# Where eight row blocks of weight sums are made, and where two squares are taken, in a fused attention and gating layer

## The chip, the cores and the metric

The kernel runs on one core of one Trainium2 chip. The metric is the device time of one launch in microseconds (us), lower is better, and the median of three runs is given. A time taken with the hardware profiler comes from one further execution of its own.

## The reference, cut to what matters

One layer of a trunk with 512 tokens of width 2048, all in float32:

```
hn = rmsnorm(x, norm_g)
q, k, v, gate = split(hn @ w_in)
out = sliding-window attention(q, k, v, with a bias by distance and a sink per head)
x = x + (out * silu(gate)) @ w_out
emb = p @ ple_proj
g = sigmoid(rmsnorm(x, ple_norm) @ ple_gate)
x = x + emb * g
return rmsnorm(x, final_g)
```

`w_out` and `ple_gate` are 2048 x 2048. The change is about the product with `ple_gate`: how some of its weights come about, and when the sums of squares for the norm ahead of it are taken.

## The kernel before, in words

**Products in three passes.** Every float32 operand is split in two: a high part (a cast on ScalarE, ACT) and a low part (a subtraction on VectorE, DVE). A product is then three matmuls: high by high, high by low, low by high (`mm3`, L126 to L128). The weights of `w_out` and `ple_gate` come as blocks of 128 x 1024 numbers, 512 KB each. A block is loaded by SyncE (SP, L757), cast by ACT into `bhi` (L765) and subtracted by DVE into `blo` (L766); then TensorE (PE) uses it in twelve matmuls, or six for the small products. A load of `w_out` goes to one of three buffers (`braw`, tag `wraw`), so it can only be issued when the block three places earlier has been split.

**Six products instead of eight.** The products with `w_out` and with `ple_gate` each multiply 2 x 2 quarters by a scheme that needs seven products of sums of quarters, of which six, numbered 1, 7, 6, 5, 3, 4 in the order of `ORDER_OUT` and `ORDER_PLE`, are done at full size and the seventh by the same scheme again at half size (`Small`). Each product runs over two column halves `jj` and, for each, over four blocks `m`. So a place in the work is written (p, jj, m): (1, 1, 2) is product 1, right columns, third block.

**Sums of weights.** Some products need sums of two or three weight quarters. These are made by DMA, not by an engine: a plain copy from DRAM to DRAM on SP's queue, then a transfer that adds another block to it, on GpSimd's queue (POOL). This goes on all through attention (`sums_in`, `sum_weights`, L723 and L725), up to two copies and two additions in each of 64 iterations `i`. For `ple_gate` there is a second way: the sums of product 7 are loaded from DRAM into eight buffers in SBUF (`seed`, tag `grown`); when product 7 has used such a block, POOL issues a transfer that adds a quarter to the same buffer in place (`grow`, L742), which gives the block of product 6, and later in the same way that of product 4. For the four blocks of product 6's right columns (jj = 1) the kernel before makes the sums in DRAM as well, by copies and additions spread over products 6 and 5 of the `w_out` stage (L1411 and L1414); they are then only loaded over the old block (`again`, L744).

**Stages.** The input projections run interleaved with attention, one iteration of the loop at about 5.6 us, up to about 450 us of the span. Then follows the `w_out` stage up to about 621, and the `ple_gate` stage up to the end. In attention all engines run in the order of the code. In the `w_out` stage PE and SP do, and ACT, DVE and POOL are ordered by the framework's scheduler; from product 4 of `w_out` on ACT is in the code's order too, and from product 7 of `ple_gate` on all are.

**Attention's end.** An iteration `i` has on POOL a small copy (L504), the selection of part of the weights of an earlier iteration (`own`, L575), then the additions of `sum_weights`. The last addition is in iteration 63, the loop runs to iteration 66, and after it POOL issues the first load of `x` (L1027).

**Squares of x.** Once a tile of 128 x 512 of the new `x` is complete, its squares are summed on ACT (L1040). Twelve of the sixteen are put off and taken one at a time at fixed places: four in product 4 of `w_out`, two in (1, 1, 2) and (1, 1, 3) of `ple_gate`, four in (7, 1, 0) to (7, 1, 3), two in (6, 0, 0) and (6, 0, 1). In each place of the stage the order on ACT is: the splits of blocks up to two ahead; then `todo`, with turned tiles scaled into `hT` (L1092), forms of the left operand (`fhg`, L881), a square if one is due; then the forms and blocks of a small product.

Of the kernel before, what the change touches and what calls it, by code (L numbers as in the profile page):

```python
# [11 lines left out]
F32 = mybir.dt.float32  # L12
F32R = mybir.dt.float32r
AF = mybir.ActivationFunctionType
ALU = mybir.AluOpType
# [5 lines left out]
P = 128  # L21
# [34 lines left out]
def trunk_kernel(ctx: ExitStack, tc: tile.TileContext, a: dict):  # L56
    nc = tc.nc
# [28 lines left out]
    WE = 1024  # L86
# [71 lines left out]
    def run(gen):  # L158
        for _ in gen:
            pass  # L160
# [38 lines left out]
    for k in range(KC):  # L199
# [54 lines left out]
        else:  # L254
            high()
            if k == 1:
                src = xw[:, w_at[512] : w_at[512] + 256]
# [9 lines left out]
        f, e = k == 0, k == KC - 1  # L267
# [416 lines left out]
    summed, copies, adds = {}, [], []  # L684

    def block(nm, r, c, jj, m):

        r = r if nm == "w_out" else 3 - r
        return a[nm][2 * (c - 1) + jj, 4 * (r - 1) + m]
# [3 lines left out]
    MORE = {7: (2, 2), 5: (1, 2), 6: (1, 1), 4: (2, 1)}  # L693
# [18 lines left out]
                copies.append((t, block(nm, *BASE[p], jj, m) if p in (7, 5) else summed[nm, BASE[p], jj, m]))  # L712
                adds.append((t, block(nm, *MORE[p], jj, m)))
    sum_small("ple_gate", 4)
    for m in range(4):
        summed["ple_gate", 6, 1, m] = tc.dram_tile([P, WE], F32, name=f"ple_gate_6_1_{m}")
    SUM_STEPS = 2 * len(copies) + 6
    SUMS_EARLY = 16

    def sum_weights(i):  # L720

        if i % 2 == 0 and i // 2 < len(copies):
            nc.sync.dma_start(*copies[i // 2])  # L723
        elif i % 2 == 1 and 0 <= i // 2 - 3 < len(adds):
            nc.gpsimd.dma_start(*adds[i // 2 - 3], accum_op=ALU.add, max_dma_last_dim=8192)  # L725
# [191 lines left out]
    blocks = TWOS * UNITS  # L917

    def sums_in(i):
# [6 lines left out]
        n, of = SUM_STEPS - SUMS_EARLY, blocks - 4  # L926
        return range(SUMS_EARLY + (i - 4) * n // of, SUMS_EARLY + (i - 3) * n // of)

    left = KC * (len(kinds) - 1)

    def some(of, n=1):
# [4 lines left out]
    for i in range(blocks + 3):  # L936

        before, softmax = softmax, scores(i) if i < blocks else iter(())
        turned = turn(i - 2) if 2 <= i < blocks + 2 else iter(())
        value = weigh(i - 3) if 3 <= i else iter(())  # L940
        next(turned, None)
        next(value, None)
        next(softmax, None)
        next(turned, None)
        next(before, None)
        next(softmax, None)
        first_chores(i, 0)
        if i in (6, 20, 36):
            idle.extend(make_key(1 + i // 16))
        todo = left // (blocks + 2 - i) if i < blocks + 2 else 0  # L950
        left -= todo
        for n in range(max(todo, 6)):
            if n < todo:
                next(proj)
            if n == 0:
                first_chores(i, 1)
                some(W.todo)
                some(chores or idle)
            elif n == 2:
                next(turned, None)  # L960
                next(value, None)
                if len(chores) > 1:
                    some(chores)
            elif n == 3:
                next(softmax, None)
            elif n == 4:
                first_chores(i, 2)
                some(chores or idle)
            elif n == 5:
                next(softmax, None)  # L970
        if i < blocks:
            for n in sums_in(i):
                sum_weights(n)
    for _ in proj:
        pass
    while chores or idle:
# [57 lines left out]
    squares_due = []  # L1034
# [338 lines left out]
    sum_copies = [(6, 0, 1), (6, 1, 0), (6, 1, 3), (5, 0, 2)]  # L1373
    sum_adds = [(6, 0, 3), (6, 1, 2), (5, 0, 1), (5, 1, 0)]
# [8 lines left out]
    for n, p in enumerate(ORDER_OUT):  # L1383
        if p == 4:
            last_out.enter_context(
                tc.manual_schedule(
                    engines={getattr(mybir.EngineType, v) for v in ("PE", "SP", "Activation")}
                )
            )
        nxt = out_forms.steps(ORDER_OUT[n + 1]) if n < 5 else iter(())  # L1390
        for jj in range(2):
            later.extend(held.pop(waiting.get((p, jj)), ()))
            calls = iter(range(4))

            def between(m, ps):
                if (p, jj, m) in EMBED_AT:
                    embedding.slot()
                q = small_steps.get((p, jj, m))
                if q is not None:
                    small_out.prepare(q)  # L1400
                for q in SMALL["w_out"].get((p, jj), {}).get(m, ()):
                    small_out.product(q)

            def todo():
                step = next(calls)
                part = x_at.get((p, jj, step))
                if part is not None:
                    load_x(part, nc.sync)
                if (p, jj, step) in sum_copies:
                    m = sum_copies.index((p, jj, step))  # L1410
                    nc.sync.dma_start(summed["ple_gate", 6, 1, m], summed["ple_gate", 7, 1, m])  # L1411
                if (p, jj, step) in sum_adds:
                    m = sum_adds.index((p, jj, step))
                    nc.gpsimd.dma_start(  # L1414
                        summed["ple_gate", 6, 1, m], block("ple_gate", *MORE[6], 1, m), accum_op=ALU.add, max_dma_last_dim=8192
                    )
                part = embed_steps.get((p, jj, step))
                if part is not None:
                    embedding.prepare(part)
                next(nxt, None)  # L1420
                if p == 4:
                    turns_due((p, jj, step))
                    if (jj, step) in ((0, 1), (0, 2), (0, 3), (1, 0)) and squares_due:
                        squares_due.pop(0)()
                if (p, jj) == (4, 1):
                    for _ in range(2 if step >= 2 else 0):
                        turn(*turns.pop(0), "o")
                        next(ple_first, None)

            ps = unit(p, jj, at_out, out_forms, todo, between)  # L1430
            posts = [partial_of(add_y, p, jj, tb, ps[tb]) for tb in range(2)]
            if p == 1:
                held[p, jj] = posts
            elif (p, jj) == (3, 1):
                later.insert(0, lambda both=posts: [post() for post in both])
            else:
                later.extend(posts)
        run(nxt)
        if p == 3:
            turns = [(kp, 0) for kp in range(4)]  # L1440
# [143 lines left out]
    for n, p in enumerate(ORDER_PLE[:-1]):  # L1584
# [9 lines left out]
        for jj in range(2):  # L1594
            calls = iter(range(4))

            def todo():
                nonlocal root_due, fg
                step = next(calls)
                k = early.get((p, jj, step))  # L1600
                if (p, jj, step) in embed_loads:
                    load_embeds(*embed_loads[p, jj, step])
                while small_due:
                    small_due.pop(0)()
                if (p, jj, step) == (5, 0, 2):
                    assert len(moves) == 4
                    while moves:
                        moves.pop(0)()
                if (p, jj, step) == (5, 0, 3):
                    for square in moved.pop(0):  # L1610
                        square()
                if (p, jj, step) == (3, 1, 0):
                    fg = late.tile([P, D], F32, tag="fg", name="fg")
                    nc.sync.dma_start(fg, a["final_g"].partition_broadcast(P))
                if p in (1, 7):
                    turns_due((p, jj, step))
                if (p, jj) == (1, 0):
                    return
                if (p, jj, step) != (7, 0, 0):
                    next(nxt, None)  # L1620
                if p == 1:
                    next(nxt, None)
                if (p, jj, step) == ROOT_AT[0]:
                    assert not squares_due
                    nc.vector.tensor_reduce(ss2, ssq2, axis=AX.X, op=ALU.add)
                    root_due = power_of_mean(rstd2, ss2, "r2")
                    next(root_due)
                if (p, jj, step) == ROOT_AT[1]:
                    run(root_due)
                if (p, jj, step) == (1, 1, 3):  # L1630
                    soon[6] = ple_forms.steps(6)
                    next(soon[6])
                if squares_due and (p == 1 and step > 1 or (p, jj) in ((7, 1), (6, 0))):
                    squares_due.pop(0)()
                if (p, jj, step) == (7, 1, 1):
                    nc.scalar.activation(ss2[:, :1], power[:, :1], AF.Sigmoid)
                if k is not None:
                    split_last(k)
                if (p, jj, step) in opens:
                    open_bank(*opens[p, jj, step])  # L1640
# [30 lines left out]
    f = ple_forms.made[4]  # L1671
# [166 lines left out]
```

## Time and profile before

| | us |
|---|---|
| median of three runs | 781.54 |
| the three runs | 781.34, 781.54, 782.19 |
| the profiled execution, its own time | 781.97 |
| span in that profile, first to last instruction | 780.3 |
| ACT busy, DVE busy, POOL busy | 531.0, 618.9, 169.9 |

The span is what the trace shows, and 781.97 - 780.3 = 1.67 us lie around it. The granted clock of TensorE has a mean of 0.997. Places in the trace are given in us from the span's start. The page of the profile has a line of busy time per engine, tenths of busy time in 40 slices, the DMA queues (q1 carries what SP issues, q0 what POOL issues), the chain of work that ended last, and groups of instructions; further views list who waited for whom, the instructions of an engine in order of time, and busy times and DMA share of chosen stretches. A number in square brackets behind an instruction is the idle time of its engine before it, with what ended it.

### The profile page before, as it was taken

The page shows a single profiled execution, that of the slowest core. Times are in us where ns is not written, and L with a number is a line of the kernel's source. Part 1 is how long each engine was busy: PE and PEld are TensorE (multiplying, and loading weights), DVE is VectorE, ACT ScalarE, POOL GpSimd, SP SyncE. Part 2 cuts the span into 40 slices and gives each one's busy share as a digit, 9 for nine tenths or more (in the row PEclk, how much of TensorE's full clock was granted, in tenths as well). Part 3 has the DMA queues.
Part 4 walks back from the last instruction along what each step waited for, and adds up shares of the span by engine and source line. Part 5 has one row for each costly group of instructions (what it writes and reads, how often), then busy time and mean ns, then how long its engine had stood idle before and what let it go on. Part 6 is the DMA issues. An engine that isn't in the chain of part 4 may idle for free.

```text
span 780.3 us, 11154 instructions
## 1 busy us (share of the span) xinstructions
PE 770.5 (99%) x3652; PEld 644.2 (83%) x3652; DVE 618.9 (79%) x1069; ACT 531.0 (68%) x1121; POOL 169.9 (22%) x307
## 2 busy tenths in 40 slices
PE   9999999999999999999999999999999999999995
PEld 8888888888888888888888888888888888888884
DVE  4556697876978688777877799968799889998995
ACT  6753586766777676766766664577766888866974
POOL 0200523132232313132332200112111122221111
PEclk9999999999999999999999999999999999999998
DMA  8988899999999989999998588999899999999956
GB/s 346 298 216 295 181 275 308 267 307 258 287 250 284 273 238 281 273 279 272 256 285 216 137 304 314 343 300 302 307 388 336 311 292 282 332 258 304 331 135 216
DMA packets 52858, 217.22 MB, mean 278 GB/s; under 512 B 8112, under 2 KB 9136, under 8 KB 46720
## 3 DMA queue, kind: packets, MB, share of 16 engines
q1 hardware_dynamic: 39280, 156.67, 56.5%
q0 software_dynamic: 13520, 59.83, 36.6%
q8 instruction: 29, 0.48, 0.2%
q14 instruction: 29, 0.24, 0.1%
HBM read 199.65 MB, written 82.89 MB: 362 GB/s over the span
## 4 chain that ended last, share of the span: by engine, by line
PE 96%; issue 1%; DMA 1%; ACT 1%; DVE 0%; POOL 0%; POOLq 0%; DVEq 0%; ACTq 0%
PE gps L126 7%; PE gps L127 7%; PE gps L128 7%; PE qps L126 7%; PE qps L128 7%; PE qps L127 7%; PE o L127 6%; PE o L126 6%; PE o L128 6%; PE g L127 4%; PE g L128 4%; PE g L126 4%; PE s L485 2%; PE vps L290 2%; PE o L603 2%; PE pt L551 2%
## 5 line engine op out<-in xcount | busy, mean ns | idle before, releaser
L766 DVE TENSOR_TENSOR blo<-braw,bhi 128x1024 fp32r<-128x1024 f32 x100 | 121.6, 1220 | 21.1 <-ACT bhi L765 20.2
L765 ACT CAST bhi<-braw 128x1024 fp32r<-128x1024 f32 x100 | 105.3, 1054 | 45.1 <-PE o L128 15.0
L126 PE MATMUL gps<-xh,whi 128*128 128x512 f32 x256 | 100.0, 390 | 0.0
L127 PE MATMUL gps<-xl,whi 128*128 128x512 f32 x256 | 99.9, 390 | 0.0
L128 PE MATMUL gps<-xh,wlo 128*128 128x512 f32 x256 | 99.8, 390 | 0.0
L126 PE MATMUL qps<-xh,whi 128*128 128x512 f32 x224 | 87.8, 392 | 0.0
L128 PE MATMUL qps<-xh,wlo 128*128 128x512 f32 x224 | 87.5, 390 | 0.0
L127 PE MATMUL qps<-xl,whi 128*128 128x512 f32 x224 | 87.4, 390 | 0.0
L575 POOL TENSOR_SCALAR_AFFINE_SELECT own<-r 64x512 fp32r<-64x512 f32 (+1 forms) x48 | 32.5, 676 | 238.3 <-DVE r L565 236.1
L110 DVE TENSOR_TENSOR wlo<-wraw,whi 128x1024 fp32r<-128x1024 f32 x60 | 73.5, 1227 | 2.9 <-ACT whi L109 2.7
L126 PE MATMUL o<-bhi,fho 128*128 128x512 f32 x192 | 74.8, 390 | 0.0
L127 PE MATMUL o<-blo,fho 128*128 128x512 f32 x192 | 74.7, 389 | 0.0
L128 PE MATMUL o<-bhi,flo 128*128 128x512 f32 x192 | 74.7, 389 | 0.0
L109 ACT CAST whi<-wraw 128x1024 fp32r<-128x1024 f32 x60 | 62.4, 1042 | 4.6 <-issue 4.1
L127 PE MATMUL g<-blo,fhg 128*128 128x512 f32 x160 | 62.4, 390 | 0.2 <-DVE blo L766 0.2
L126 PE MATMUL g<-bhi,fhg 128*128 128x512 f32 x160 | 62.3, 390 | 0.0
L128 PE MATMUL g<-bhi,flg 128*128 128x512 f32 x160 | 62.3, 389 | 0.0
L128 PEld LDWEIGHTS gps<-xh,wlo 128*128 128x128 f32 x256 | 48.1, 188 | 10.2
L529 ACT ACTIVATE t<-t,sm 128x129 f32<-128x129 f32 (+1 forms) x128 | 50.0, 392 | 8.6 <-DVE sm L525 7.3
L126 PEld LDWEIGHTS gps<-xh,whi 128*128 128x128 f32 x256 | 48.1, 188 | 9.1
L127 PEld LDWEIGHTS gps<-xl,whi 128*128 128x128 f32 x256 | 48.1, 188 | 8.9
L565 DVE TENSOR_TENSOR r<-pt,r 128x256 fp32r<-128x256 f32 x56 | 23.7, 424 | 38.7 <-ACT r L564 37.9
(299 smaller groups left out, 1829.3 us busy)
## 6 DMA issues: line engine op xcount, KB each, us to landing
wraw<-in_w_gate_in SPq DMA_DIRECT2D x32, 512.0 KB, 8.1
w_out<-in_w_out POOLq DMA_DIRECT2D x32, 512.0 KB, 9.1
braw<-w_out SPq DMA_DIRECT2D x32, 512.0 KB, 7.2
wraw<-in_w_q SPq DMA_DIRECT2D x28, 512.0 KB, 6.6
braw<-in_w_out SPq DMA_DIRECT2D x22, 512.0 KB, 5.7
braw<-in_ple_gate SPq DMA_DIRECT2D x22, 512.0 KB, 7.1
ple_gate<-in_ple_gate POOLq DMA_DIRECT2D x20, 512.0 KB, 8.8
xw<-in_first SPq DMA_DIRECT2D x14, 640.5 KB, 6.6
```

The source lines that it names most:

```text
L109: nc.scalar.copy(hi, raw)
L110: nc.vector.tensor_sub(lo, raw, hi.bitcast(F32))
L126: nc.tensor.matmul(ps, sh, mh, start=first, stop=False, skip_group_check=more)
L127: nc.tensor.matmul(ps, sh, ml, start=False, stop=False, skip_group_check=more)
L128: nc.tensor.matmul(ps, sl, mh, start=False, stop=last, skip_group_check=more)
L290: nc.tensor.matmul(v_ps[t], h[:, c], part_of(high_at, 256, 512), start=f, stop=e, skip_group_check=True)
L485: nc.tensor.matmul(s_ps[:, u, : 2 * n], st, of_keys[:, first * 2 * QB : (first * QB + n) * 2], start=True, stop=True)
L529: nc.scalar.activation(su, su, AF.Exp, bias=sm[:, u : u + 1], accum_out=sm[:, 2 + u : 3 + u])
L565: nc.vector.tensor_sub(rl, src, rh.bitcast(F32))
L575: nc.gpsimd.affine_select(out=flat(own), in_=flat(r).bitcast(F32), pattern=[[0, 8], [sign, HB]], compare_op=ALU.is_ge, fill=0.0, base=-HB ...
L765: nc.scalar.copy(hi[:, :n], raw)
L766: nc.vector.tensor_sub(lo[:, :n], raw, hi[:, :n].bitcast(F32))
```

## The change

The four blocks of product 6's left columns (jj = 0) are now made in DRAM too. Their copies are issued by SP at the end of iterations 61 and 62, two in each, and the additions by POOL at the end of iterations 63 to 66, one in each. Since these blocks are then in `summed`, `add_stage` gives them the kind `again`: the four transfers that added to a buffer in place become four plain loads on the same queue. The right columns' copies and additions stay where they were, by way of two new functions. And the two squares of the first product go from steps 2 and 3 of (1, 1) to steps 0 and 3: the first moves two blocks earlier, the second stays. (For (1, 0) `todo` returns before that line.)

```
-    for m in range(4):
-        summed["ple_gate", 6, 1, m] = tc.dram_tile([P, WE], F32, name=f"ple_gate_6_1_{m}")
+    for jj in range(2):
+        for m in range(4):
+            summed["ple_gate", 6, jj, m] = tc.dram_tile([P, WE], F32, name=f"ple_gate_6_{jj}_{m}")
+
+    def copy_six(jj, m):
+        nc.sync.dma_start(summed["ple_gate", 6, jj, m], summed["ple_gate", 7, jj, m])
+
+    def add_six(jj, m):
+        src = block("ple_gate", *MORE[6], jj, m)
+        nc.gpsimd.dma_start(summed["ple_gate", 6, jj, m], src, accum_op=ALU.add, max_dma_last_dim=8192)
+
...
+    six_copied = {blocks - 3: (0, 1), blocks - 2: (2, 3)}
+    six_added = {blocks - 1: (0,), blocks: (1,), blocks + 1: (2,), blocks + 2: (3,)}
...
         if i < blocks:
             for n in sums_in(i):
                 sum_weights(n)
+        for m in six_copied.get(i, ()):
+            copy_six(0, m)
+        for m in six_added.get(i, ()):
+            add_six(0, m)
...
-                if squares_due and (p == 1 and step > 1 or (p, jj) in ((7, 1), (6, 0))):
+                if squares_due and (p == 1 and step in (0, 3) or (p, jj) in ((7, 1), (6, 0))):
                     squares_due.pop(0)()
```

More of the change, by code (lines that the diff above doesn't have):

```diff
@@ L1409, in todo @@
                 if (p, jj, step) in sum_copies:
-                    m = sum_copies.index((p, jj, step))
-                    nc.sync.dma_start(summed["ple_gate", 6, 1, m], summed["ple_gate", 7, 1, m])
+                    copy_six(1, sum_copies.index((p, jj, step)))
                 if (p, jj, step) in sum_adds:
[L1413 to L1416, printed above, removed]
+                    add_six(1, sum_adds.index((p, jj, step)))
                 part = embed_steps.get((p, jj, step))
```

## The prediction

> **What bounds the kernel now.** I read the page first, then the list of who waited for whom, cut to PE, then the chain that ended last.
>
> ```profile
> PE 770.5 (99%) x3652; PEld 644.2 (83%) x3652; DVE 618.9 (79%) x1069; ACT 531.0 (68%) x1121; POOL 169.9 (22%) x307
> ```
>
> ```profile
> PE g L127 <- DVE blo L766: 0.2, 1, 0.2
> ```
>
> ```profile
> 765.00:780.30 15.30, 6.49 (x51) 6.19 (x50) 7.50 (x18) 5.28 (x11) 1.24 (x3) 0.86 0.52 188
> ```
>
> PE is busy for 770.5 of the 780.3 us. Of the 9.8 us that are left, 15.30 - 6.49 = 8.8 lie in the last stretch, after the last matmuls, and most of the rest ahead of the first one. Between them the list names one single wait of PE, 0.2 us, for a low part of weights (`blo`). So an edit that takes no matmul out can win that one wait and little else, while anything that comes too late for PE is paid in full. The rows around it are these, from PE, ACT and DVE in order of time:
>
> ```profile
> 641.29 0.39 PE L126 MATMUL g<-bhi,fhg 128*128 128x512 f32 x1
> 644.01 0.39 PE L126 MATMUL smallg<-bhi,small_ahg 128*128 128x512 f32 x1
> 645.37 0.39 PE L126 MATMUL g<-bhi,fhg 128*128 128x512 f32 x1
> 645.92 0.50 PE L127 MATMUL g<-blo,fhg 128*128 128x512 f32 x1 [0.16 <-DVE blo L766]
> ```
>
> ```profile
> 634.40 0.64 ACT L1163 ACTIVATE small_ahg<-hT 128x512 fp32r<-128x512 f32 x1
> 634.94 1.05 ACT L765 CAST bhi<-braw 128x1024 fp32r<-128x1024 f32 x1
> 638.07 1.05 ACT L765 CAST bhi<-braw 128x1024 fp32r<-128x1024 f32 x1 [1.56 <-DMA braw<-in_ple_gate]
> 642.93 0.63 ACT L1040 ACTIVATE s<-x1s 128x512 f32<-128x512 f32 x1
> 643.56 1.04 ACT L765 CAST bhi<-grown 128x1024 fp32r<-128x1024 f32 x1
> ```
>
> ```profile
> 636.02 1.23 DVE L766 TENSOR_TENSOR blo<-braw,bhi 128x1024 fp32r<-128x1024 f32 x1 [0.18 <-ACT bhi L765]
> 643.17 1.29 DVE L882 TENSOR_TENSOR flg<-hT,fhg 128x512 fp32r<-128x512 f32 x2
> 644.64 1.23 DVE L766 TENSOR_TENSOR blo<-grown,bhi 128x1024 fp32r<-128x1024 f32 x1 [0.18 <-ACT bhi L765]
> ```
>
> Twelve matmuls, one block, take 644.01 - 641.29 = 2.72 us, so one every 0.227. The wait stands where product 7 begins: its first matmul is at 645.37, its second, which needs the low part, at 645.92, 0.55 later and so 0.32 late. The low part came from DVE at 644.64, DVE had waited for the cast at 643.56, and ahead of that cast ACT had taken a square, at 642.93. That square is the one that the change moves.
>
> **The squares.** The first one goes from (1, 1, 2) to (1, 1, 0), where ACT's order puts it straight ahead of the small product's form at 634.40. It takes 643.56 - 642.93 = 0.63 us of ACT. The casts behind it shift by that much, and at 638.07 ACT waits 1.56 us for a load, which swallows it. Who waits for them: the low part at 636.02 would come at about 636.65 and be done at 637.9, for a matmul in the block that starts at 641.29 - 2.72 = 638.57 and needs it 0.23 later: 0.9 us to spare. If that cover were gone it would cost at most 0.63. The squared tile has long been complete: the last addition to `x` is an earlier instruction of DVE, at 614.82, by the same view.
>
> ```profile
> 614.82 0.68 DVE L1120 TENSOR_TENSOR x1s<-smallo,x1s 128x512 f32<-128x512 f32 x1
> ```
>
> What is late next: the cast comes at 642.93 instead of 643.56, but DVE is held by the two forms until 643.17 + 1.29 = 644.46. So its subtraction starts at 644.46 instead of 644.64, 0.18 us earlier, and of the 0.32 us 0.14 stay. I take a gain of 0.18. The bounds: 0, if DVE's order changes for the worse, and 0.32, the whole wait. The second square stays where it was.
>
> **The four transfers of the `ple_gate` stage.**
>
> ```profile
> grown<-in_ple_gate POOLq DMA_DIRECT2D x12, 512.0 KB, 9.4
> grown<-ple_gate POOLq DMA_DIRECT2D x4, 512.0 KB, 8.2
> ```
>
> ```profile
> 646.44 0.95 POOL L742 DMA_DIRECT2D grown<-in_ple_gate  x1 [6.07 <-issue]
> 654.43 0.87 POOL L742 DMA_DIRECT2D grown<-in_ple_gate  x1 [1.85 <-DVE blo L766]
> ```
>
> The four that add in place are issued from 646.44 to 654.43. They become plain loads like the other four, whose median from issue to landing is 8.2 us instead of 9.4. Nothing waits for either: their blocks are split from 675.94 on, 21 us after the last issue, and PE has no wait behind 645.92. So the 1.2 us each, and whatever room the DMA rings gain, are worth 0. They begin behind the one wait of PE and cannot touch it.
>
> ```profile
> 675.94 1.06 ACT L765 CAST bhi<-grown 128x1024 fp32r<-128x1024 f32 x1
> ```
>
> **The copies, at attention's end.** SP's rows put them behind the last two loads of projection weights.
>
> ```profile
> 414.10 5.76 SPq L102 DMA_DIRECT2D wraw<-in_w_gate_in  x2
> ```
>
> ```profile
> 433.62 1.04 ACT L109 CAST whi<-wraw 128x1024 fp32r<-128x1024 f32 x1
> ```
>
> Two go out just after 414.10 and two just after the second load, at about 419.9. What they read was finished in iteration 45, by the order of `sum_weights`, so SP doesn't wait. Behind the first two stands the load of 419.5, which ACT casts at 433.62, 14 us later; behind the others only the first loads of `w_out`, for a product that starts at 450.44 (row below). No row has such a copy alone. From below it is a plain load, 0.52 MB at the 411 GB/s of a full stretch (460 to 462.5, below), 1.3 us of all rings; from above an addition, which reads more, at 2.96 (next). Two copies are then 2.6 to 5.9 us in front of a load that needs some 5 and has 14. Cost 0, at either end.
>
> **The additions, at attention's end.** POOL's rows, and one addition with little beside it:
>
> ```profile
> 434.26 0.80 POOL L725 DMA_DIRECT2D small_ple_gate<-in_ple_gate  x1
> 446.59 1.58 POOL L575 TENSOR_SCALAR_AFFINE_SELECT own<-r 128x512 fp32r<-128x512 f32 x1 [6.62 <-DVE r L565]
> 450.55 0.83 POOL L1027 DMA_DIRECT2D x1s<-in_x  x1 [2.38 <-PE o L603]
> ```
>
> ```profile
> q0 software_dynamic: 80, 0.52, 29.6%
> ```
>
> The last row is the stretch 435 to 445, in which q0 carries a single addition: 29.6% of 10 us, 2.96 us of all sixteen rings. POOL issues the first new one behind 434.26, the second behind the selection of the next iteration, at about 440, the third and fourth behind 446.59, at about 448.2 and 449. Each holds POOL for 0.80 us and stands behind the selection of its iteration, and the load of `x` at 450.55 waited for PE anyway. On POOL itself they cost nothing. Their copies, at the 8.2 us that loads of the same sums took to landing, are in by 429.
>
> The first two fall into rings that are two thirds free. The last two, 5.92 us of ring time, meet the first loads of `w_out`:
>
> ```profile
> 447.50:450.00 2.50, 2.50 (x13) 2.07 (x12) 2.50 (x3) 1.13 (x3) 0.68 (x1) 1.00 0.54 164
> 450.00:452.50 2.50, 2.50 (x14) 2.09 (x13) 2.50 (x5) 2.45 (x5) 0.83 (x1) 1.00 0.42 75
> 452.50:455.00 2.50, 2.50 (x13) 2.06 (x11) 2.46 (x5) 2.37 (x4) 0.00 (x0) 1.00 0.84 329
> 455.00:457.50 2.50, 2.50 (x13) 2.07 (x12) 2.50 (x4) 1.05 (x1) 0.00 (x0) 1.00 0.71 277
> 457.50:460.00 2.50, 2.50 (x13) 2.07 (x12) 2.50 (x4) 1.06 (x1) 0.00 (x0) 1.00 0.66 244
> 460.00:462.50 2.50, 2.50 (x13) 2.07 (x12) 2.50 (x4) 0.96 (x1) 0.00 (x0) 1.00 1.06 411
> 470.00:472.50 2.50, 2.50 (x13) 2.07 (x12) 2.50 (x3) 1.47 (x3) 0.00 (x0) 1.00 0.58 167
> ```
>
> The last column but one is the rings' share. Free are 2.5 x (0.46 + 0.58 + 0.16 + 0.29 + 0.34) = 4.6 us from 447.5 to 460. So 5.92 - 4.6 = 1.3 us of work are pushed past 460, where the rings are full, and are taken up by 472.5 (2.5 x 0.42 = 1.05 us free in the last row, the rest ahead of it). Does PE notice 1.3 us? The block whose cast waited for a load inside that time, and its low part:
>
> ```profile
> 470.71 1.06 ACT L765 CAST bhi<-braw 128x1024 fp32r<-128x1024 f32 x1 [0.60 <-DMA braw<-w_out]
> ```
>
> ```profile
> 472.62 1.23 DVE L766 TENSOR_TENSOR blo<-braw,bhi 128x1024 fp32r<-128x1024 f32 x1
> ```
>
> ```profile
> 450.44 0.40 PE L126 MATMUL o<-bhi,fho 128*128 128x512 f32 x1
> ```
>
> Counting blocks from 0 at 450.44, block 9 needs its low part at 450.44 + 9 x 2.72 + 0.23 = 475.15. It had it at 472.62 + 1.23 = 473.85, and DVE started 0.85 after the cast had ended at 471.77, so its load may come 0.85 + 1.30 = 2.15 us later. Later blocks come when the backlog is gone. Hence cost 0, with 2.15 - 1.3 = 0.85 us of cover. If it goes, every further us is one of PE.
>
> Sum for the profiled execution: 781.97 - 0.18 = 781.8. Against the median of the runs, 0.43 lower: 781.54 - 0.18 = 781.4.
>
> A rule that speaks against the change. In rows: memory moved
>
> ```profile
> HBM read 199.65 MB, written 82.89 MB: 362 GB/s over the span
> ```
>
> and the change adds four copies (read and write) and four additions (two reads, one write), 20 x 0.524 = 10.5 MB. The addition above moved three times 0.52 MB in 2.96 us, 530 GB/s of reads and writes together, so the span's mean is no ceiling here. The Trainium skill's "HBM Reference", section "Specifications (TRN2)", gives a core some 358 GB/s. The trace goes beyond it, and the section itself says that a core alone does. By that ceiling the last two additions would take 8.8 us, and by the working of the second rival below the result would be some 783.4.
>
> **The rivals.** A measurement of this kernel can tell about 0.2%, 1.56 us, from no change.
>
> *The additions take the place of loads (slower).* Queue q0 is served ahead of q1, so that the first `w_out` loads find no free time: 5.92 us late at block 9, less 2.15, is 3.8 us of PE: 781.4 + 3.8 = 785.2. It decides from a delay of 2.15 us on, and is slower by 0.2% from 2.15 + 1.56 + 0.18 = 3.9. Against it: with additions in flight a load took 4.8 us, and 3.9 in the next stretch, nearly without:
>
> ```profile
> braw<-in_w_out SPq DMA_DIRECT2D x4, 512.0 KB, 4.8
> ```
>
> ```profile
> braw<-in_w_out SPq DMA_DIRECT2D x4, 512.0 KB, 3.9
> ```
>
> That is 0.9 us for an addition or two. Chance 0.08: 0.06 beyond 0.2%, 0.02 within.
>
> *Memory is the ceiling (slower).* At the span's mean of 362 GB/s the 3.15 MB of the last two additions take 8.7 us, 4.1 more than the free 4.6; less block 9's 2.15 that is 1.9 us: 783.3. The 530 GB/s speak against it. Chance 0.02.
>
> *A scheduler's order (slower).* ACT and DVE in the `w_out` stage are ordered by the framework, which now sees other transfers. An addition to `x` (0.68 us) ahead of a low part with 1.3 us to spare costs nothing, a third one 0.7, three such places 2.2: 783.6. Nothing in the profile speaks for it. Chance 0.03, 0.02 of it beyond 0.2%.
>
> *The square does nothing.* DVE takes other work in the 0.18 us, or the load behind the wait at 638.07 lands later: 781.5. Chance 0.12.
>
> *Faster by over 0.2%.* PE's waits between the start and the last stretch hold 0.32 us, so only the tail of 8.8 us could give it, and no edit touches that. Chance 0.02.
>
> **How the numbers follow.** The forecast, all hidden but 0.18 us, has 0.73 and gives 781.4. Same: 0.73 + 0.12 + 0.02 + 0.01 = 0.88; slower 0.06 + 0.02 + 0.02 = 0.10; faster 0.02. The range goes down by the 0.14 us of the wait that may go too and 0.2 of the runs' spread below their median, to 781.0, and up by 0.65 of the spread above it and 0.85 for a collision that goes a little past its cover, to 782.9. Left out are the 0.10 and 0.02 beyond 0.2%.
>
> **What would show it.** Right: PE's list of waits keeps at most the 0.2 us, now below 0.15, ACT's cast of the first `grown` block comes straight behind the forms with no square ahead, and the span shrinks by 0.1 to 0.3. The rows of POOL at 446 to 455 give way to loads of 0.54 us of issue, and the stretch 440 to 450 has more DMA share. Wrong: waits of PE for `blo` between 455 and 485, with casts waiting for `braw<-w_out` over 2 us longer than now, or a wait of PE at a new place of the first product, which would be the square at its new step.

## The result, and the profile after

The changed kernel takes 783.27 us (median of 22 runs, 781.85 to 784.87); beside it the kernel before took 782.17 (22 runs, 781.34 to 782.82). The ratio is 1.0014, with a 95% interval of 1.0008 to 1.002: slower, by about 1.1 us, within the 0.2% that I had called the limit of what can be told from one measurement, but outside my range, which ended at 782.9. The profiled execution took 782.67 us, with a span of 781.0.

The page's line of busy times has hardly moved (PE 770.9 us, 770.5 before).

Who waited for whom, cut to PE (us in total, times, the longest), without the wait at its start that both kernels have: the wait at the start of product 7 of `ple_gate` is gone, and one in the `w_out` stage has come (`blo` is made at L775 now, L766 before).

```profile
PE o L127 <- DVE blo L775: 0.7, 1, 0.7
```

Where the time went is read from three marks of PE in order of time: the first matmul of `w_out`, the first of `ple_gate`, and the late one between them. Here they are of the kernel after:

```profile
450.30 0.40 PE L126 MATMUL o<-bhi,fho 128*128 128x512 f32 x1
...
466.65 0.39 PE L126 MATMUL o<-bhi,fho 128*128 128x512 f32 x1
467.74 0.50 PE L127 MATMUL o<-blo,fho 128*128 128x512 f32 x1 [0.70 <-DVE blo L775]
...
622.11 0.48 PE L126 MATMUL g<-bhi,fhg 128*128 128x512 f32 x1
```

And the first of `ple_gate` before:

```profile
620.79 0.48 PE L126 MATMUL g<-bhi,fhg 128*128 128x512 f32 x1
```

The `w_out` stage took 620.79 - 450.44 = 170.35 us before and 622.11 - 450.30 = 171.81 after, 1.46 longer. At 467.74 the low part is 467.74 - 466.65 - 0.23 = 0.86 us late; the rest is lost in steps of some 0.1 to 0.15 at the blocks behind it. The same difference for the `ple_gate` stage is 150.43 before and 150.05 after, for attention, from the first matmul of the gate projection (`gps`, 70.80 before, 70.67 after), 379.64 and 379.63. The engines' order is that of before, but for the square and the added transfers.

Back from PE to DVE and ACT, in order of time (start, duration, idle time before it in brackets), first DVE after:

```profile
462.24 1.23 DVE L775 TENSOR_TENSOR blo<-braw,bhi 128x1024 fp32r<-128x1024 f32 x1 [1.75 <-ACT bhi L774]
464.12 1.28 DVE L1138 TENSOR_TENSOR x1s<-x1s,o 128x512 f32<-128x512 f32 x2 [0.66 <-PE o L128]
...
466.47 1.22 DVE L775 TENSOR_TENSOR blo<-braw,bhi 128x1024 fp32r<-128x1024 f32 x1
```

```profile
461.15 1.05 ACT L774 CAST bhi<-braw 128x1024 fp32r<-128x1024 f32 x1 [4.08 <-DMA braw<-in_w_out]
```

```profile
450.41 0.83 POOL L1043 DMA_DIRECT2D x1s<-in_x  x1 [0.81 <-PE o L603]
```

And DVE before, at the low part of block 6:

```profile
464.00 1.22 DVE L766 TENSOR_TENSOR blo<-braw,bhi 128x1024 fp32r<-128x1024 f32 x1
```

Block 5 (counted from 0) was cast only at 461.15, because its load, issued at 453.2, took 7.8 us where it took 4.1 before. So DVE stood idle for 1.75 us, and for another 0.66 before it could use the first quarter of `x`. (The bracket at 464.12 names PE, but `x`, issued at 450.41, landed 13.6 us later, at 464.0; before, the same subtraction ran at 461.67 without a wait.) The low part of block 6 then came at 466.47, where before it came at 464.00. The issues of 445 to 465 show both late loads (KB each, median us to landing); the `w_out` loads took 3.9 before, the quarter of `x` 5.7 by the same view:

```profile
braw<-in_w_out SPq DMA_DIRECT2D x4, 512.0 KB, 7.4
ple_gate<-in_ple_gate POOLq DMA_DIRECT2D x2, 512.0 KB, 9.4
x1s<-in_x POOLq DMA_DIRECT2D x1, 1024.0 KB, 13.6
```

The busy times by stretch of 2.5 us, after. The last two columns are the rings' share and what they moved:

```profile
447.50:450.00 2.50, 2.50 (x13) 2.07 (x12) 2.50 (x3) 1.26 (x3) 2.10 (x3) 1.00 0.64 205
450.00:452.50 2.50, 2.50 (x14) 2.13 (x13) 2.50 (x5) 2.45 (x5) 0.83 (x1) 1.00 0.64 131
452.50:455.00 2.50, 2.50 (x13) 2.07 (x12) 2.45 (x5) 2.22 (x4) 0.00 (x0) 1.00 0.95 157
455.00:457.50 2.50, 2.50 (x13) 2.07 (x12) 2.50 (x4) 1.06 (x1) 0.00 (x0) 1.00 0.95 233
457.50:460.00 2.50, 2.50 (x13) 2.07 (x12) 2.50 (x4) 0.00 (x0) 0.00 (x0) 1.00 0.99 387
460.00:462.50 2.50, 2.50 (x13) 2.07 (x12) 0.76 (x2) 1.05 (x1) 0.00 (x0) 1.00 1.01 397
```

Two things stand out. From 452.5 to 457.5 the rings were 95% taken and yet moved 157 and 233 GB/s, where before they moved 329 and 277 at a lower share. And the columns of DVE in these rows and in those of the prediction: before, DVE was busy 2.50 of 2.50 us in nearly every one. It had no free time in which to make good a delay.

### The profile page after: what moved, and what is told of

Its sections match the earlier page's. It is cut to its first block, busy times and chain, and to the rows that moved or that the text cites. A ratio compares the mean times of both kernels' runs of the same rounds, so it can differ in the third digit from the quotient of the medians.

```text
span 781.0 us, 11165 instructions
## 1 busy us (share of the span) xinstructions
PE 770.9 (99%) x3652; PEld 643.7 (82%) x3652; DVE 618.5 (79%) x1069; ACT 529.0 (68%) x1121; POOL 171.1 (22%) x311
## 4 chain that ended last, share of the span: by engine, by line
PE 98%; issue 1%; DVE 0%; POOL 0%; POOLq 0%; DVEq 0%
PE gps L126 7%; PE gps L127 7%; PE gps L128 7%; PE qps L126 7%; PE qps L127 7%; PE qps L128 7%; PE o L127 6%; PE o L128 5%; PE o L126 5%; PE g L126 5%; PE g L128 5%; PE g L127 5%; PE s L485 2%; PE vps L290 2%; PE o L603 2%; PE pt L551 2%
## 5 line engine op out<-in xcount | busy, mean ns | idle before, releaser
L775 DVE TENSOR_TENSOR blo<-braw,bhi 128x1024 fp32r<-128x1024 f32 x100 | 121.5, 1220 | 22.0 <-ACT bhi L774 21.2
L564 ACT CAST r<-pt 128x256 fp32r<-128x256 f32 x56 | 20.9, 372 | 49.8 <-PE pt L551 49.3
```

Of the source, the lines that this page charges most:

```text
L564: nc.scalar.copy(rh, src)
L775: nc.vector.tensor_sub(lo[:, :n], raw, hi[:, :n].bitcast(F32))
```

## The experiments

*Theory A*: the third and fourth addition share the rings with the load of block 5 and with the first quarter of `x`; DVE idles, and since it is fully busy up to about 480, its idle time goes on to PE, less what DVE is ahead. *Theory B*: what costs is `x` alone, whose load stands behind the two additions on POOL's queue. Other rivals are named where they are tested. The result of each kernel stands beside the kernel before on the same chip (781.9 for the first four, 781.79 for the next four, 781.72 for the last four), and "stage" is the `w_out` stage as worked out above.

**The square alone**, in the kernel before:

```
-                if squares_due and (p == 1 and step > 1 or (p, jj) in ((7, 1), (6, 0))):
+                if squares_due and (p == 1 and step in (0, 3) or (p, jj) in ((7, 1), (6, 0))):
```

> The kernel before with the moved square alone. In the profile of after PE's wait at the start of gate product 7 is gone, 0.55 + 0.10 us of late matmuls where I had forecast that 0.14 would stay, so all theories of the loss expect PE's last matmul about 0.4 us earlier than in the kernel before and a time 0.4 us lower, with no wait of PE between 450 and 485. If the square at its new step costs something that the sums hid, it shows here as a wait of PE between 631 and 645.

781.75 us, ratio 0.9997 (0.9988 to 1.0006). The stages are 379.64, 170.35 and 149.98 (150.43 for the last one before), and PE has no wait in any. The square's move costs nothing and brings nothing that can be measured.

**The sums alone**: the changed kernel with the square's line as before.

> The change without the moved square. If the loss comes from the additions at the end of attention, PE waits about 1.3 to 1.5 us for low parts at the head of the w_out stage (460 to 480), keeps its old wait at 645, and the time is 1.4 us above the kernel before. If the loss came from the square or from the four loads of the gate stage, the waits at 460 to 480 would be gone and the time within 0.3 us of before.

783.37 us, 1.0019 (1.001 to 1.0028), stage 172.36. The low part is later still, and DVE idles 1.94 and 0.99 us. DVE's rows:

```profile
462.63 1.23 DVE L775 TENSOR_TENSOR blo<-braw,bhi 128x1024 fp32r<-128x1024 f32 x1 [1.94 <-ACT bhi L774]
464.85 1.28 DVE L1138 TENSOR_TENSOR x1s<-x1s,o 128x512 f32<-128x512 f32 x2 [0.99 <-DMA x1s<-in_x]
```

The sums carry the loss. With the square in its old place, product 7 has no wait here either.

**x ahead of the two additions**, in the changed kernel:

```
-    six_added = {blocks - 1: (0,), blocks: (1,), blocks + 1: (2,), blocks + 2: (3,)}
+    six_added = {blocks - 1: (0,), blocks: (1,)}
...
+    with tc.manual_schedule(engines={mybir.EngineType.Pool}):
+        load_x(0, nc.gpsimd)
+        for m in (2, 3):
+            add_six(0, m)
```

> The change with the third and fourth addition issued behind the first load of x on GpSimd's queue instead of ahead of it. Theory A (shared rings): the load of w_out's sixth block, issued at 453.2, still shares the rings with both additions; its cast stays at 460.5 or later, DVE, which has no free time from 450 to 480, idles 1.5 us or more, and PE loses at least 0.4 us. Theory B (x behind the additions): what costs is that the first quarter of x lands at 464 instead of 456, so that DVE's subtraction from x, ahead of the seventh block's low part, waits 0.66 us; x lands at about 458 here, that wait is gone, PE loses nothing, and the time is 0.3 to 0.4 us below the kernel before. Both together: DVE's idle time falls from 2.4 to 1.7 us, and PE's loss from 1.4 to about 0.5.

784.18 us, 1.003 (1.0021 to 1.0038), stage 172.55: more than in the changed kernel. `x` now takes 5.8 us to land, as before the change, but the additions come later and hold up block 5 the more, whose load takes 9.3 us (7.8 in the changed kernel):

```profile
464.11 1.23 DVE L775 TENSOR_TENSOR blo<-braw,bhi 128x1024 fp32r<-128x1024 f32 x1 [3.25 <-ACT bhi L774]
```

Theory B falls: with `x` in time the loss is larger. In the changed kernel `x` has its share, the 0.66 us, but it isn't the cause alone. One idle time of 3.25 us costs the stage 2.20.

**The sums five iterations earlier**, in the changed kernel:

```
-    six_copied = {blocks - 3: (0, 1), blocks - 2: (2, 3)}
-    six_added = {blocks - 1: (0,), blocks: (1,), blocks + 1: (2,), blocks + 2: (3,)}
+    six_copied = {blocks - 8: (0,), blocks - 7: (1,), blocks - 6: (2,), blocks - 5: (3,)}
+    six_added = {blocks - 4: (0,), blocks - 3: (1,), blocks - 2: (2,), blocks - 1: (3,)}
```

> The change with the copies in iterations 56 to 59 and the additions in 60 to 63, so that the last addition is issued at about 435 and lands by 446. Both theories A and B: no addition is in flight when w_out's loads and x begin, PE has no wait from 450 to 485, the gain of the square stays, and the time is 0.4 us below the kernel before. If instead the added traffic of 10.5 MB is what costs, wherever it is put, loads of projection weights come late for PE between 400 and 445 and the time is again 1 us above before.

783.53 us, 1.0022 (1.0014 to 1.0031), stage 171.03. I had expected no cost, and missed. Most of it lies in attention now, which takes 381.32, 1.68 more; the `w_out` stage is 0.68 longer, without idle time of DVE between 450 and 480. Rings that were 0.70 to 0.90 taken from 420 to 440 are full there (one stretch is shown; its share was 0.70 before), the first `w_out` block comes late, and ACT, which takes things in the code's order, is late with all that stands behind it, down to a cast of attention (`own`) that PE waits for (451.31 here, 448.21 before). The stretch, PE's list, and ACT:

```profile
425.00:430.00 5.00, 5.00 (x27) 4.22 (x26) 2.98 (x8) 1.31 (x5) 2.41 (x5) 1.00 1.07 261
```

```profile
PE o L605 <- ACT own L585: 1.2, 2, 1.0
```

```profile
442.38 1.05 ACT L774 CAST bhi<-braw 128x1024 fp32r<-128x1024 f32 x1 [2.07 <-DMA braw<-in_w_out]
...
451.31 0.41 ACT L585 CAST own<-own 64x256 fp32r<-64x256 f32 x1 [1.84 <-POOL own L575]
```

So the rings' free time in attention doesn't hold four additions at these places; two of them, at about 434 and 440, it does (next).

**Two blocks only**: the changed kernel with blocks 0 and 1 alone made in DRAM, so that the first two additions stay and the last two go.

```
-    six_copied = {blocks - 3: (0, 1), blocks - 2: (2, 3)}
-    six_added = {blocks - 1: (0,), blocks: (1,), blocks + 1: (2,), blocks + 2: (3,)}
+    six_copied = {blocks - 3: (0, 1)}
+    six_added = {blocks - 1: (0,), blocks: (1,)}
```

> The change for the first two blocks of the left columns alone: two copies at the end of iteration 61 and the additions of iterations 63 and 64; blocks three and four are again added to in place. Theory A (the rings, shared with the third and fourth addition, starve w_out's sixth block): from its first w_out matmul to the first of the gate stage PE takes 170.35 us as in the kernel before, no wait at 460 to 480, and with the moved square the time is 0.1 to 0.4 us below before. Rival (the whole 10.5 MB counts wherever it falls): about half of the change's loss of 1.5 us stays in that stage, 0.7 us.

781.91 us, 0.9999 (0.999 to 1.0008), stage 170.36. The first two blocks are free, as forecast.

**The two late additions alone**, in the kernel before, with nothing else of the change (what they add to is copied in iterations 48 and 50):

```
+        if i in (blocks + 1, blocks + 2):
+            m = i - blocks - 1
+            nc.gpsimd.dma_start(
+                spare_sums[m], block("ple_gate", *MORE[6], 0, m), accum_op=ALU.add, max_dma_last_dim=8192
+            )
```

> The kernel before with nothing but two extra additions at the places of the change's third and fourth, into two blocks of DRAM that were copied in iterations 48 and 50 and that nothing reads; old square, old gate stage. Theory A: these two alone give the loss, 1.2 to 2.0 us of waits for low parts at 460 to 480, x's first quarter 13 us to landing, and a time 1.2 to 2 us above before. Rival (the copies and the first two additions fill the end of attention and push work past 447, without which the late two would fit): at most 0.5 us of wait, time within 0.5 us of before.

782.84 us, 1.0014 (1.0005 to 1.0022), stage 171.50. That is the whole loss of the change. DVE:

```profile
462.18 1.23 DVE L767 TENSOR_TENSOR blo<-braw,bhi 128x1024 fp32r<-128x1024 f32 x1 [1.58 <-ACT bhi L766]
463.62 1.28 DVE L1131 TENSOR_TENSOR x1s<-x1s,o 128x512 f32<-128x512 f32 x2 [0.22 <-DMA x1s<-in_x]
469.12 1.22 DVE L767 TENSOR_TENSOR blo<-braw,bhi 128x1024 fp32r<-128x1024 f32 x1 [0.21 <-ACT bhi L766]
```

**The sums in the `w_out` stage**: the changed kernel with copies and additions of the left columns in products 5 and 3 of `w_out`, beside those of the right ones.

```
+    left_copies = [(5, 0, 3), (5, 1, 1), (5, 1, 3), (3, 0, 1)]
+    left_adds = [(5, 1, 1), (5, 1, 3), (3, 0, 1), (3, 0, 3)]
```

> The change with the four copies and additions of the left columns moved into the w_out stage, right behind those of the right columns: copies at (5,0,3), (5,1,1), (5,1,3), (3,0,1), additions at (5,1,1), (5,1,3), (3,0,1), (3,0,3), about 535 to 560 us. The rings are as full there as at 460 (shares of 0.9 to 1.0), but from product 6 on a block is loaded five places ahead into eight buffers instead of three ahead into three. If what a transfer costs is decided by how long before its use the load beside it was issued, PE sees nothing: attention 379.6, w_out stage 170.35 to 170.5, gate stage 150.0, time 0.1 to 0.4 us below before. If the rings' total work decides, the w_out stage is 1 us or more longer, as when the sums were put five iterations earlier in attention.

790.15 us, 1.0111 (1.0095 to 1.0126), stage 178.54: 8.19 longer, and far from both of my cases (nothing, and "1 us or more"). On POOL each addition waits for its copy (one for 5.49 us, the one shown for 10.48), and the stores of embeddings, which free buffers for SP's loads, stand behind it: SP waited 37.7 us in all for these stores, 30.1 before. POOL, then the longest entry of PE's list:

```profile
575.22 0.83 POOL L724 DMA_DIRECT2D ple_gate<-in_ple_gate  x1 [10.48 <-DMA ple_gate<-ple_gate]
```

```profile
PE smallo L126 <- ACT bhi L774: 2.7, 1, 2.7
```

A wait on an in-order queue costs those behind it; the rings are not the only thing to look at.

**The kernel before, once more.**

> The kernel before once more, for a second profile: how firm PE's one wait at the start of gate product 7 is. If it comes from the square, as I forecast, it is there again, 0.3 to 0.45 us, and the gate stage takes 150.4 us. If it comes from loads that happened to land late in the one profile (ACT had waited 1.56 and 0.21 us for them), it is smaller or gone: 150.0 us, as in the run of the sums alone, which had the old square and no wait.

One execution, 781.97 us; stages 379.64, 170.35 and 149.98. In this profile, with the square in its old place, product 7 of `ple_gate` has no wait.

**Two late plain copies** in place of the two late additions, at the same place on the same queue, with the same two copies in iterations 48 and 50:

```
+            nc.gpsimd.dma_start(spare_sums[m], block("ple_gate", *MORE[6], 0, m), max_dma_last_dim=8192)
```

> The kernel before with two spare transfers on GpSimd's queue at the ends of iterations 65 and 66, as in the run with two late additions alone, but plain copies of 512 KB from DRAM to DRAM in place of additions (nobody reads them). Theory A (the ring time of the additions delays the sixth load of w_out and x's first quarter, and DVE has about 0.95 us to spare): a plain copy takes under half of the rings' time of an addition, so DVE idles by at most 1 us between 450 and 480, the w_out stage stays at 170.35 to 170.6 us, and the time is that of before, within 0.3 us. Rival (any two transfers at this place on this queue hold back x's quarter and the load by standing ahead of them, whatever they do): as with the two additions, stage at 171.5, time 1.0 to 1.2 us above before.

781.75 us, 1.0 (0.9991 to 1.0008), stage 170.36, no idle time of DVE up to 480. So it isn't that two transfers stand ahead of `x`. The issues of 445 to 465, and one of the stretches:

```profile
q0 software_dynamic: 432, 2.10, 29.1%
...
braw<-in_w_out SPq DMA_DIRECT2D x4, 512.0 KB, 4.5
...
spare_sums<-in_ple_gate POOLq DMA_DIRECT2D x2, 512.0 KB, 5.1
x1s<-in_x POOLq DMA_DIRECT2D x1, 1024.0 KB, 7.1
```

```profile
452.50:455.00 2.50, 2.50 (x13) 2.07 (x12) 2.45 (x5) 2.45 (x5) 0.00 (x0) 1.00 0.95 300
```

The same view of the two additions and of before:

```profile
q0 software_dynamic: 432, 2.10, 44.7%
```

```profile
q0 software_dynamic: 272, 1.05, 16.1%
```

Of 20 us, with the load of `x` taken as before (3.2 us), the two copies took 0.291 x 20 - 0.161 x 20 = 2.6 us of all rings, 1.3 each, and the two additions 0.447 x 20 - 3.2 = 5.7, 2.9 each, for the same bytes by the queue's count.

**x late alone**: the kernel before with the load of the first quarter held on POOL until the low part of the fourth block is made.

```
-    load_x(0, nc.gpsimd)
...
+                if (p, jj, step) == (1, 0, 1):
+                    lo = B.made[at_out[1, 0][3]][1][0]
+                    nc.gpsimd.tensor_copy(x1[0][:, 0, 0:1], lo[:, 0:1].bitcast(F32))
+                    load_x(0, nc.gpsimd)
```

> The kernel before with the load of x's first quarter held back on POOL until the low part of the fourth block of w_out is made, at about 457, and no added transfers. Theory A: x's quarter lands at about 463 to 464, as in the changed kernel, but the loads of w_out are in time; DVE idles at most once, by under 1 us, and the w_out stage is longer by 0 to 0.3 us. Rival B (lateness of x alone is what costs): DVE idles by over 1.5 us and the stage is longer by 1 to 1.5 us.

787.07 us, 1.0069 (1.0057 to 1.0082), stage 175.15. The experiment overshot: the load was issued at 458.82 and took 10 us, so `x` came at 468.9 and not at 463 to 464, and neither theory's number applies. DVE idled 5.29 us and PE waited 2.89:

```profile
468.90 0.69 DVE L1122 TENSOR_TENSOR x1s<-x1s,o 128x512 f32<-128x512 f32 x1 [5.29 <-DMA x1s<-in_x]
```

```profile
467.50 0.39 PE L126 MATMUL o<-bhi,fho 128*128 128x512 f32 x1
470.78 0.66 PE L127 MATMUL o<-blo,fho 128*128 128x512 f32 x1 [2.89 <-DVE blo L766]
471.24 0.63 PE L128 MATMUL o<-bhi,flo 128*128 128x512 f32 x1
471.67 0.63 PE L126 MATMUL o<-bhi,fho 128*128 128x512 f32 x1
```

It shows that `x` can hold DVE too, when it is late enough. What a lateness of `x` as small as in the change would cost by itself is left open by it; that `x` isn't the cause alone was shown by the kernel with `x` ahead.

**One late addition** instead of two.

> The kernel before with one spare addition, at the end of iteration 65, instead of two (nobody reads it). Theory A: half the ring time, DVE idles by 0 to 1 us between 450 and 480, and since about 0.95 us are to spare the w_out stage is longer by 0 to 0.2 us: no difference that can be measured. Rival (each addition costs its share from the first on): half of what two cost, 0.5 to 0.7 us.

781.86 us, 1.0001 (0.9992 to 1.001), stage 170.36, though DVE idles:

```profile
461.61 1.23 DVE L767 TENSOR_TENSOR blo<-braw,bhi 128x1024 fp32r<-128x1024 f32 x1 [0.93 <-ACT bhi L766]
```

**The changed kernel, once more.**

> The changed kernel once more, for how much the loss differs from one execution to the next. Theory A: the w_out stage at 171.3 to 172.4 us (two kernels with the same transfers gave 171.81 and 172.36), with DVE idle about 0.95 us longer than the loss, and no wait of PE at the start of product 7 of ple_gate. Rival (the square's move decides the 0.5 us between those two): 171.81 within 0.1.

One execution, 782.18 us, stage 170.82. I had expected at least 171.3, so the loss varies more than I thought, and this time the `ple_gate` stage has the old wait, though the square is moved: it takes 150.39, and product 7's second matmul is 0.28 us late. DVE and PE:

```profile
461.62 1.22 DVE L775 TENSOR_TENSOR blo<-braw,bhi 128x1024 fp32r<-128x1024 f32 x1 [1.05 <-ACT bhi L774]
463.01 1.29 DVE L1138 TENSOR_TENSOR x1s<-x1s,o 128x512 f32<-128x512 f32 x2 [0.16 <-DMA x1s<-in_x]
...
645.01 1.22 DVE L775 TENSOR_TENSOR blo<-grown,bhi 128x1024 fp32r<-128x1024 f32 x1
```

```profile
645.77 0.39 PE L126 MATMUL g<-bhi,fhg 128*128 128x512 f32 x1
646.28 0.50 PE L127 MATMUL g<-blo,fhg 128*128 128x512 f32 x1
```

Put in order by DVE's idle time between 450 and 480, the profiles give one line:

| kernel | DVE idle, us | stage longer by, us |
|---|---|---|
| before (twice), square alone, two blocks, plain copies | 0 | 0 to 0.01 |
| one late addition | 0.93 | 0.01 |
| changed, once more | 1.05 + 0.16 = 1.21 | 0.47 |
| two late additions alone | 1.58 + 0.22 + 0.21 = 2.01 | 1.15 |
| changed | 1.75 + 0.66 = 2.41 | 1.46 |
| sums alone | 1.94 + 0.99 = 2.93 | 2.01 |
| `x` ahead | 3.25 | 2.20 |

Some 0.7 to 1.05 us of idle time are free, and each further us is one of the stage. Theory A holds, and the loss differs between executions of one kernel as the idle time does. Three kernels are left out of the table, because their stage lost time in other ways too: the one with `x` late holds a slower clock, as told at the end, and another order of DVE's work (a product for `gate` comes ahead of the subtraction from `x`); those with the sums five iterations earlier and in the `w_out` stage have no idle time of DVE between 450 and 480, and lose elsewhere.

## Why the prediction was wrong

**What bounds the kernel.** Right: what the changed kernel loses is low parts that come late for PE, and it is paid in full.

**The square.** Its cost of 0 was right, its gain of 0.18 not. It was one rival's case (0.12). I had taken one profile's wait for a property of the kernel. Of the fourteen profiles, seven have the square in its old place and seven have it moved, and the wait is in one of each: in the first one of the kernel before, and in the second one of the changed kernel. What sets it is the second of ACT's last two casts from `braw` ahead of product 7. Here it is in these two profiles, the kernel before first; both times it waits for its load:

```profile
639.33 1.06 ACT L765 CAST bhi<-braw 128x1024 fp32r<-128x1024 f32 x1 [0.21 <-DMA braw<-in_ple_gate]
```

```profile
639.97 1.05 ACT L774 CAST bhi<-braw 128x1024 fp32r<-128x1024 f32 x1 [0.21 <-DMA braw<-in_ple_gate]
```

DVE starts product 7's low part 5.29 to 5.31 us after this cast in all seven profiles with the old place, and 5.04 to 5.05 in all seven with the new one. So the move does make the low part earlier, by 0.26 us, more than the 0.18 forecast. But PE is held up only when this cast is late: it came 645.37 - 639.33 = 6.04 us ahead of product 7 in the one profile and 645.77 - 639.97 = 5.80 in the other, and 6.10 to 6.60 in the twelve without the wait. In the first profile of the changed kernel it came 6.14 ahead; with the square in its old place the low part would have been some 0.2 us late there (an estimate from these figures: 0.32 late at 6.04, so 0.22 at 6.14). So the move is worth something only in executions with a late load. That the load's landing decides was read from these profiles, not tried by itself.

**The four transfers of the `ple_gate` stage, the copies, the first two additions.** Cost 0, right: the kernel with two blocks has all of these kinds and shows no loss. The price of a copy, 1.3 us, and of an addition, 2.96, taken from the nearest rows, were right too: 1.3 and 2.9 were measured.

**The last two additions.** Here it failed, at the step "So 5.92 - 4.6 = 1.3 us of work are pushed past 460" and at the one behind it, the tolerance of "block 9". First, the free time of a stretch isn't filled just because work is there. By the rows, the rings were taken for 2.5 x (0.54 + 0.42 + 0.84 + 0.71 + 0.66) = 7.9 us from 447.5 to 460 before and for 2.5 x (0.64 + 0.64 + 0.95 + 0.95 + 0.99) = 10.4 after: the rings did 2.5 us more work, so of the 5.9 us 3.4, not 1.3, went past. Until 452.5 the rings stood at 0.64 while the additions were in flight. Second, the balance at 460 was the wrong one to draw: block 5's load goes out at 453.2 into rings full of additions, and it is the first to be late, not block 9. Third, the 2.15 us of tolerance were one block's, counted as if DVE could take other work in the meantime and be back in time. But DVE had no free time at all, as the rows that I quoted showed in the third column of busy times, which I didn't read. Idle time at block 5 shifts everything behind it. From 464.00 to 472.62 DVE takes three blocks in 8.62 us, 2.87 each, PE needs one every 2.72: DVE falls back by 0.15 a block and can't catch up. What was really to spare is the 475.15 - 473.85 = 1.30 us of block 9's low part; measured were 0.7 to 1.05.

**The rivals.** "The additions take the place of loads" was the right mechanism, with its size wrong: 5.92 us late at block 9 and 785.2 were priced, and it came as 2.41 us of idle time at blocks 5 and 6, and 1.46 us of PE. Not all of the loads' time was taken: they landed in 7.4 us rather than 3.9. I had argued against it with loads that took 4.8 us beside "an addition or two"; two additions one right behind the other did what single ones, 5 us apart, didn't. One late addition alone made the loads 5.6 us, and that was still free.

"Memory is the ceiling" comes near by its number, 783.3, but not by its mechanism: the profiles count 201.74 MB read and 84.99 written both for the two additions and for the two plain copies, and the copies took 1.3 us of the rings each where the additions took 2.9. Read and written, a copy is 1.05 MB, 806 GB/s over 1.3 us. The counts hold one read and one write for an addition, where I had reckoned with two reads; even with those, 1.57 MB in 2.9 us is 542 GB/s, less than a copy reaches. The Trainium skill's "HBM Reference", section "Specifications (TRN2)", has some 358 GB/s for a core, by which, as an estimate, two copies alone would hold the rings for 5.9 us; the trace disagrees, and so the 783.4 by that figure was near by luck too. The scheduler's order was out: it did not change.

**The numbers.** The range's upper end allowed 0.85 us for a collision beyond the runs' spread. Needed were 783.27 - 782.17 = 1.10 and the 0.18 of gain that did not come, 1.28. Beside that, 781.54 was low among the medians of the kernel before: 781.72 to 782.17 in the later measurements. From 782.17 the same working would have put the range's end at 783.5, beyond what was measured; but the way of the change, a gain of 0.18, would have been wrong even so.

## What to carry to other kernels

Whether a delay is paid is read from the engine that passes it on: look at that engine's busy column over the stretch, and if it is full, add up its idle times and compare them with its lead, not with the slack of one instruction. Draw the balance of the DMA rings at the moment when each load is issued, for work that is in front of it then, and don't count as free what comes after. A single wait of a few tenths of a us in a single profile may be that execution's and not the kernel's: take a second profile before a gain is worked out from it.

## What the runs showed of the hardware

An addition from DRAM to DRAM fills the rings with little to show for it: 2.9 us of all sixteen for 0.52 MB, against 1.3 for a plain copy of the same block, with the rings at 0.95 moving 157 GB/s in one stretch (300 beside the copies, at the same share). Why it takes so long is not shown here.

A wait of PE of about 3 us costs more than itself. Behind the 2.89 us wait of the kernel with `x` late, matmuls came every 0.43 us instead of 0.23 (471.24 and 471.67 above), and the stretches show why (the column ahead of the DMA share is the granted clock):

```profile
469.00:470.78 1.78, 0.00 (x1) 0.00 (x1) 1.78 (x3) 1.40 (x2) 0.00 (x0) 1.00 1.04 388
470.78:472.00 1.22, 1.22 (x3) 1.03 (x4) 1.22 (x3) 0.00 (x0) 0.00 (x0) 0.57 0.68 175
472.00:473.00 1.00, 1.00 (x4) 0.72 (x4) 1.00 (x2) 0.00 (x0) 0.00 (x0) 0.50 0.81 246
474.00:475.00 1.00, 1.00 (x6) 0.77 (x5) 1.00 (x3) 0.04 (x1) 0.00 (x0) 0.82 0.00 0
```

From 470.78 on some nine matmuls came 0.2 us slower each, about 1.7 us lost behind a gap of 470.78 - 467.50 - 0.23 = 3.05. In the kernel with the sums in the `w_out` stage the 2.7 us wait, which ended at 574.5, was followed by the same:

```profile
574.00:576.00 2.00, 1.02 (x2) 0.51 (x3) 1.50 (x2) 0.99 (x2) 0.78 (x2) 0.50 1.00 346
```

Behind the changed kernel's wait of 0.7 us the clock stayed at 1.00. The Trainium skill's "TensorE: Matmul & The Clock Gate", section "What's actually happening", has the half clock come after an idle window of about 3.4 us; the two waits here were shorter and enough.
